# Preparing the first four delta rule heads in the front stage of a hybrid encoder layer, with keys projected later and wider steps

## Chip, cores and metric

The kernel runs on one core of one Trainium2 chip. The metric is device time in microseconds (us), the median of several runs. Engines are named as in the profile: PE is TensorE, PEld its weight load, DVE is VectorE, ACT is ScalarE, POOL is GpSimd, and SP issues most DMAs.

## What is computed

One bidirectional encoder layer over two sequences of 256 tokens, 512 rows in all, at width 1024. Three branches work side by side on the normalized input: a gated delta rule with 8 heads, latent attention (MLA) with 8 heads, and cross-attention with 4 heads into 256 memory tokens. Each is gated, projected to width 1024 and weighted by a sigmoid; the sum goes through `w_out`, and a final RMSNorm follows. Cut to what matters:

```python
h = rmsnorm(x, attn_norm_gain)
qkv, ab, z_gdn, cq, ckv, z_mla, q_mem, z_mem, gate_logits = split(h @ w_in)
q, k, v = split(silu(centred_conv(qkv, conv_w)))           # 5 taps
q, k = l2norm(q), l2norm(k)                                # per head
g, beta = -exp(a_log) * softplus(ab[0:2] + dt_bias), sigmoid(ab[2:4])
# delta rule, forward and backward, in chunks of 64 tokens:
lmat = (k*beta) @ k.T * decay, below the diagonal
t_inv = inverse(lmat + eye)
u, w = t_inv @ (v*beta), t_inv @ (k*beta*exp(gc))
for each chunk:
    v_new = u - w @ state
    o = (q*exp(g)) @ state + ((q @ k.T) * decay) @ v_new
    state = state*exp(g_last) + (k*exp(g_last - g)).T @ v_new
o_gdn = rmsnorm(o_fwd + o_bwd) * silu(z_gdn)
o_mla = mla(cq, ckv) * silu(z_mla)
o_mem = softmax(q_mem @ k_mem.T) @ v_mem * silu(z_mem)
merged = sum(sigmoid(gate_i) * (o_i @ w_branch_i))
y = rmsnorm(x + merged @ w_out, final_norm_gain)
```

## The kernel before, in words

Features lie on the 128 partitions and the 512 tokens along the free dimension. Each f32 operand of a large product is split into a rounded high part and a low rest, and the product is three passes on PE: high by high, high by low, low by high. `weight` (L190) loads a weight tile of 512 KB over SP, rounds it on ACT (`wh`, L200) and subtracts on DVE, or on POOL for the q, k and v tiles (`wl`, L204). `gemm` (L231) then runs 24 matmuls of 128x128 by 512 columns. `split` (L210, L212) does the same to activations.

There are three stages. The front stage (`front`, L1286) projects the memory keys and values, normalizes x, and runs the attention of the memory heads and of the eight MLA heads. In the attention of one head, s is a matmul (L281); DVE takes the maximum (L284, L290), ACT the exponential p (L295), DVE the reciprocal and the division of p (L298, L300); PE transposes p (pt, L304) and multiplies by v. Between these steps `fills(n)` takes whole tiles of other work from a list that `plan` (L1255) writes: projections of the delta rule's q, k and v with the convolution behind them (`qkv_tile`: five taps on DVE, L685 and L687, the last with SiLU), tokens of v transposed (`v_tokens`, with the copy vt on ACT, L710), merge gates g, output gates z.

The middle stage (`middle`, L1326) runs the delta rule. Its PE order is set by the program itself: `weave` drives several generators, which yield the PE time of a step and the time until the next is ready, and fills the gaps with tiles from what is left of the list. The generators are `preps`, `heads_load`, `heads_in`, two lanes of solves and `heads_out`. All other engines get an order from a scheduler that goes by priorities and its own clock.

`gdn_prep` (L714) prepares four heads at once: exponents of the decay (dr, ed, L735 to L742), products of keys in blocks of 32 (kd, 256 small matmuls, L753), norms, and the inverse of 32x32 blocks by a recurrence on DVE. That has 31 steps, each a product and a sum over the result of all steps before:

```python
nc.vector.tensor_tensor(t3, xx[:, i:i+1, 0:i].to_broadcast([P, i, i]), tt[:, 0:i, 0:i], op=ALU.mult)   # L800
nc.vector.tensor_reduce(tt[:, 0:i, i], t3, axis=AX.X, op=ALU.add)                                      # L802
```

Transposes (L810, L812) and copies on ACT to t32 (L823) and y32 (L826, L830) follow. In the middle stage of before, both groups of four heads are prepared there. For each head, `decay_in` and the exponentials of the decay e are made and multiplied with k by k (kk, L901; e, L912). `gdn_solve` then goes through a chain of small matmuls with copies between: p (L952) from t32, yp (L964), y (L977, L981), x (L995), u (L1005), xs (L1015), w (L1019), us (L1024), and the copies ub (L1010, L1027). `gdn_out` makes the output o (L1048) and its norm (so, L1064).

The back stage projects the delta rule's branch and multiplies by `w_out` (L1172); the last half row ends in a chain over DVE, ACT and POOL (L1178 to L1222).

At the very start, `mem_v` loads memT and the parameters prm. `add_square` (L241, L244) squares memT on ACT, and `split` multiplies it by a gain out of prm (mh, L210) for the first matmul vm (L358).

Of the kernel before, what the change touches and what calls it, by code (L numbers as in the profile page):

```python
# [7 lines left out]
F32 = mybir.dt.float32  # L8
F32R = mybir.dt.float32r
# [4 lines left out]
P = 128  # L14
# [140 lines left out]
class Layer:  # L155
# [16 lines left out]

    def ta(self, name):
        return self.pk.tile([P, 512], F32, tag="ta", bufs=2, name=name)
# [15 lines left out]
    def weight(self, src, n, name, pool=None):  # L190
# [9 lines left out]
        nc.scalar.activation(hi[:, :n], raw[:, :n], AF.Copy)  # L200
# [6 lines left out]
    def split(self, src, hi, lo, scale=1.0):  # L207

        nc = self.nc
        nc.scalar.activation(hi, src, AF.Copy, scale=scale)  # L210
        if isinstance(scale, float) and scale == 1.0:
            nc.vector.tensor_tensor(lo, src, hi.bitcast(F32), op=ALU.subtract)  # L212
        else:
            nc.vector.scalar_tensor_tensor(lo, src, scale, hi.bitcast(F32), ALU.mult, ALU.subtract)

# [110 lines left out]
    def mem_v(self):  # L326
# [6 lines left out]
        with self.tc.high_priority(offset=1000):  # L333
            for k in range(8):
                raw = self.pa.tile([P, 512], F32, tag="K", bufs=8, name=f"memT{k}")
# [8 lines left out]
        for k, (raw, wr) in enumerate(raws):  # L344
# [7 lines left out]
            self.split(raw, hl[:, 0], hl[:, 1], self.mg[:, k:k + 1])  # L352
# [7 lines left out]
            self.add_square(acc, raw, k, 1)  # L360
# [21 lines left out]
    def mem_kt(self, h):  # L382
# [5 lines left out]
            hi = self.pa.tile([P, 512], F32R, tag="K", bufs=8, name=f"kmh{h}")  # L388
            lo = self.pa.tile([P, 512], F32R, tag="K", bufs=8, name=f"kml{h}")
# [251 lines left out]
    def mla_qk(self, hh, between):  # L641
        A = self.A
        r = []
        for w, nk, xs, n, tag, bufs in ((A["w2"], 2, self.kl, "kn", "K", 8), (A["w3"], 3, self.ql, "qn", "Qn", 4)):
# [3 lines left out]
            hi = self.pa.tile([P, 512], F32R, tag=tag, bufs=bufs, name=f"{n}h{hh}")  # L648
            lo = self.pa.tile([P, 512], F32R, tag=tag, bufs=bufs, name=f"{n}l{hh}")
# [39 lines left out]
    def qkv_tile(self, h, part):  # L689
# [4 lines left out]
        if part < 2:  # L694
            if part == 0:
                self.kq[h] = self.pk.tile([P, 2, 2, 256], F32, tag="kq", bufs=8, name=f"kq{h}")
            self.conv(ps, f, self.kq[h][:, :, part], f"{f}")
            return
# [4 lines left out]
    def v_tokens(self, h):  # L703
# [6 lines left out]
        nc.scalar.activation(vt, vp, AF.Copy)  # L710
# [3 lines left out]
    def gdn_prep(self, g, kqs):  # L714
# [4 lines left out]
        nc = self.nc  # L719
        pg, c = self.pg, self.c  # L720
        h0 = 4 * g

# [23 lines left out]
        kp = self.ps_ms(0, f"kd{g}")  # L746
        for h in range(4):
            for s in range(2):
                for cc in range(2):
                    w = h * 4 + s * 2 + cc  # L750
                    for a in range(4):
                        t = slice(cc * P + 32 * a, cc * P + 32 * a + 32)
                        nc.tensor.matmul(kp[32 * a:32 * a + 32, 32 * w:32 * w + 32],  # L753
                                         kqs[h][:, s, 0, t], kqs[h][:, s, 0, t], start=True, stop=True)
# [37 lines left out]
        yield 1.8, 0.0  # L792
# [4 lines left out]
        for i in range(1, 32):  # L797
# [9 lines left out]
        if g:  # L807
            yield 0.0, 4.0
# [4 lines left out]
        if g:  # L813
            yield 0.0, 4.0


        t32 = pg.tile([P, 16, 32], F32, tag="t32", bufs=2, name=f"t32{g}")

        y32 = pg.tile([P, 32, 32], F32, tag="y32", bufs=2, name=f"y32{g}")
        for a in range(4):  # L820
# [3 lines left out]
            if g:  # L824
                yield 0.0, 1.5
        nc.scalar.activation(y32[:, 0:16], o2[:, :, 0:16].rearrange("p i u -> p u i"), AF.Copy)  # L826
        if g:
            yield 0.0, 2.5
        for q in range(2):
            nc.scalar.activation(y32[:, 16 + q:32:2], o1[:, :, 17 - q:32:2].rearrange("p i u -> p u i"), AF.Copy)  # L830
            if g:
                yield 0.0, 1.5
        self.ready[g] = self.now + (10 if g else 80)
# [37 lines left out]
    def gdn_in(self, hh):  # L871
# [8 lines left out]
        self.decay_exp(hh, 0, es[0])  # L880
        yield 0.0, 2.0
        self.decay_exp(hh, 1, es[1])
# [10 lines left out]
        yield 0.0, 6.0  # L893
# [24 lines left out]
    def gdn_solve(self, hh):  # L918
# [37 lines left out]
        nc.scalar.activation(p1s, p1[:, 0:128], AF.Copy, scale=-1.0)  # L956
        yield 0.32, 5.0
# [11 lines left out]
        def blk(i, f, g):  # L969
            return y[32 * f:32 * f + 32, i, :, 32 * g:32 * g + 32]  # L970


        for i in range(2):
            for q in range(2):
                d = q ^ i
                for f in (2 * q, 2 * q + 1):
# [515 lines left out]
```

## Time and profile before

| | us |
|---|---|
| median of 3 runs | 892.63 (892.06 to 894.81) |
| the profiled execution | 892.01 |
| its span | 890.2 |
| PE busy | 864.7 (97%) |
| PE weight load busy | 708.5 (80%) |
| DVE busy | 588.5 (66%) |
| ACT busy | 456.9 (51%) |
| POOL busy | 205.1 (23%) |

The profile is one execution; an engine is busy while it has an instruction in work. A row of the waits gives the waiting engine and line, then the engine and line it waited for, the sum in us, how often, and the longest. A row of a group gives line, engine, operation, output and inputs, shape and count, then busy us and the mean in ns, then the idle time just before and what ended it. A row of the timeline gives start, duration, engine and operation.

### The profile page before, as it was taken

Reading aid. Unit: us, or ns where it says so; the run is one execution under the profiler, and the core shown is the slowest. Engines: PE = TensorE matmul, PEld = TensorE weight load, DVE = VectorE, ACT = ScalarE, POOL = GpSimd, SP = SyncE. Lnnn points to the kernel's source line nnn. Section 1 sums busy time; section 2 is a strip of 40 time slices with the busy share of each in tenths; the row PEclk is TensorE's granted clock in tenths of the full one; section 3 lists DMA queues with packets and bytes.
Section 4 is the critical chain, followed back from the end, with each engine's and each line's share of the span. In section 5 each row is a group of like instructions: output and inputs, shape, how many; then the busy total and the mean of one; then the engine's idle time right before and its main releaser. Section 6 shows DMA issues by size and latency. Waiting matters only on the chain. (4 is left out here: it accounts for less than half of the span.)

```text
span 890.2 us, 13288 instructions
## 1 busy us (share of the span) xinstructions
PE 864.7 (97%) x4908; PEld 708.5 (80%) x4908; DVE 588.5 (66%) x992; ACT 456.9 (51%) x879; POOL 205.1 (23%) x150
## 2 busy tenths in 40 slices
PE   7999999999999999999998999999999999999996
PEld 5878886878888878887777877778888888888885
DVE  6775437876678775589996998775665544435642
ACT  6655455545554454456359557686665442213332
POOL 0230340121221310063330214422220001432121
PEclk9999999999999999999999999999999999999999
DMA  9322221542225423465341346434343337365332
GB/s 329 125 77 94 74 76 48 151 119 86 94 89 163 142 76 104 130 183 164 104 129 62 131 130 179 145 115 140 92 138 119 103 124 255 123 217 185 118 95 95
DMA packets 49313, 114.03 MB, mean 128 GB/s; under 512 B 6752, under 2 KB 12000, under 8 KB 49248
## 3 DMA queue, kind: packets, MB, share of 16 engines
q1 hardware_dynamic: 44496, 104.52, 37.5%
q10 hardware_dynamic: 4752, 8.65, 2.6%
q8 instruction: 39, 0.64, 0.3%
q14 instruction: 26, 0.21, 0.1%
HBM read 93.03 MB, written 16.97 MB: 124 GB/s over the span
## 5 line engine op out<-in xcount | busy, mean ns | idle before, releaser
L204 POOL TENSOR_TENSOR wl_qkv<-wr_qkv,wh_qkv 128x1024 fp32r<-128x1024 f32 x24 | 59.0, 2457 | 155.4 <-ACT wh_qkv L200 55.6
L685 DVE SCALAR_TENSOR_TENSOR kq<-cz,prm,kq 128x510 f32<-128x510 f32 (+1 forms) x64 | 54.2, 847 | 10.7 <-ACT kq L678 9.9
L231 PE MATMUL gm_qkv<-hh,wh_qkv 128*128 128x512 f32 x192 | 52.2, 407 | 3.2 <-DVE zt_z L1081 2.5
L231 PE MATMUL gm_g<-hh,wl_g 128*128 128x512 f32 x192 | 52.0, 400 | 0.0
L231 PE MATMUL gm_g<-hh,wh_g 128*128 128x512 f32 x192 | 51.9, 404 | 0.0
L231 PE MATMUL gm_qkv<-hh,wl_qkv 128*128 128x512 f32 x192 | 51.6, 405 | 0.0
L231 PE MATMUL gm_g<-hl,wh_g 128*128 128x512 f32 x192 | 51.3, 400 | 0.0
L231 PE MATMUL gm_qkv<-hl,wh_qkv 128*128 128x512 f32 x192 | 50.7, 399 | 0.0
L1142 POOL TENSOR_TENSOR mg<-mg,lg 128x512 f32<-128x512 f32 x16 | 29.0, 1814 | 79.4 <-DVE lg L1141 79.4
L231 PEld LDWEIGHTS gm_qkv<-hh,wh_qkv 128*128 128x128 f32 x192 | 35.3, 191 | 12.4 <-DVE zt_z L1081 3.2
L231 PEld LDWEIGHTS gm_qkv<-hl,wh_qkv 128*128 128x128 f32 x192 | 35.8, 188 | 8.6 <-issue 0.4
L231 PEld LDWEIGHTS gm_qkv<-hh,wl_qkv 128*128 128x128 f32 x192 | 35.8, 192 | 7.9
L231 PEld LDWEIGHTS gm_g<-hh,wh_g 128*128 128x128 f32 x192 | 35.3, 189 | 8.4 <-issue 0.5
L231 PEld LDWEIGHTS gm_g<-hh,wl_g 128*128 128x128 f32 x192 | 35.5, 189 | 7.7
L231 PEld LDWEIGHTS gm_g<-hl,wh_g 128*128 128x128 f32 x192 | 35.4, 189 | 7.8
L1172 PE MATMUL y<-wh_wo,mh 128*128 128x512 f32 (+1 forms) x144 | 40.0, 370 | 0.0
L200 ACT ACTIVATE wh_qkv<-wr_qkv 128x1024 fp32r<-128x1024 f32 x24 | 25.4, 1058 | 26.2 <-PE gm_qkv L231 6.5
L800 DVE TENSOR_TENSOR tm<-xx,tt 128x1 f32<-128x1 f32 (+30 forms) x62 | 37.0, 597 | 1.2
L204 DVE TENSOR_TENSOR wl_g<-wr_g,wh_g 128x1024 fp32r<-128x1024 f32 x24 | 31.3, 1306 | 9.4 <-PE gm_za L231 4.1
L200 ACT ACTIVATE wh_g<-wr_g 128x1024 fp32r<-128x1024 f32 x24 | 25.3, 1056 | 21.6 <-PE gm_g L231 12.7
L891 POOL TENSOR_TENSOR kl<-kq,kh 128x512 fp32r<-128x512 f32 x16 | 23.7, 1484 | 53.0 <-ACT kh L889 53.0
L685 DVE SCALAR_TENSOR_TENSOR vf<-cz,prm,vf 128x510 f32<-128x510 f32 (+1 forms) x32 | 29.6, 925 | 7.4 <-ACT vf L678 7.1
(403 smaller groups left out, 2263.2 us busy)
## 6 DMA issues: line engine op xcount, KB each, us to landing
wr_qkv<-in_w_dram SPq DMA_DIRECT2D x24, 512.0 KB, 3.5
wr_g<-in_w_dram SPq DMA_DIRECT2D x24, 512.0 KB, 3.6
e<-d_r SPq DMA_DIRECT2D x64, 96.0 KB, 3.5
wr_z<-in_w_dram SPq DMA_DIRECT2D x12, 512.0 KB, 3.6
wr_za<-in_w_dram SPq DMA_DIRECT2D x8, 512.0 KB, 3.4
d_g<-gt_g ACTq DMA_DIRECT2D x16, 256.0 KB, 2.0
wr_bm<-in_w_dram SPq DMA_DIRECT2D x8, 512.0 KB, 3.5
lg<-d_g SPq DMA_DIRECT2D x16, 256.0 KB, 3.4
```

What stands on the lines that cost most here:

```text
L200: nc.scalar.activation(hi[:, :n], raw[:, :n], AF.Copy)
L204: eng.tensor_tensor(lo[:, :n], raw[:, :n], hi[:, :n].bitcast(F32), op=ALU.subtract)
L231: nc.tensor.matmul(ps[:m], a[:, k * m:(k + 1) * m], xs[k][j], start=n == 0, stop=n == 3 * nk - 1)
L685: nc.vector.scalar_tensor_tensor(ys, zs, self.cw[:, f, m:m + 1], ys, ALU.mult, ALU.add)
L800: nc.vector.tensor_tensor(t3, xx[:, i:i + 1, 0:i].to_broadcast([P, i, i]), tt[:, 0:i, 0:i], op=ALU.mult)
L891: nc.gpsimd.tensor_tensor(lo, src, hi.bitcast(F32), op=ALU.subtract)
L1142: nc.gpsimd.tensor_tensor(self.merged[d], self.merged[d], gt, op=ALU.add)
L1172: nc.tensor.matmul(ps, xs[2 * j + q][a][:, t], b[:, q * 512 + c0:q * 512 + c1], start=j == 0 and n == 0, stop=j == 3 and n == 5)
```

## The change

Four things change.

The preparation of the first four heads now runs in the front stage. `front` makes the generator `prep0` ahead of the MLA heads and takes some steps of it behind each head from the second on, at lowered priority; the middle stage finishes it with the copies to t32 and y32. For this its pool pb is opened ahead of the front stage's pool, and some tiles of the front stage share tags in pb.

The list of fills has another order: k of heads 0 to 3 first, then q and v of these heads between gates; k of heads 4 to 7 is projected later, in the middle stage, and the second preparation waits for it.

The steps in the middle stage are spaced wider in the planner: 6.5 instead of 4.5 or 5.0 in the solve, 8 for 6 in `gdn_in`, 11 for 9 for the load of e; in the recurrence the spacing is narrower. Copies of y into blocks that need only y32 go ahead of yp; the copy vt gets a high priority; the exponentials come behind the last rounding of a weight.

At the two ends, the first square on ACT comes behind the rounding of mh, and in the last half row the product with the final gain moves from POOL to DVE, behind the row's factor r.

```diff
 def mem_v(self):
-            self.split(raw, hl[:, 0], hl[:, 1], self.mg[:, k:k + 1])
+            rnd = self.split(raw, hl[:, 0], hl[:, 1], self.mg[:, k:k + 1])
...
-            self.add_square(acc, raw, k, 1)
+            with self.tc.issue_after(rnd.ins) if k == 0 else nullcontext():
+                self.add_square(acc, raw, k, 1)
 def v_tokens(self, h):
-        nc.scalar.activation(vt, vp, AF.Copy)
+        with self.tc.high_priority(offset=2000):
+            nc.scalar.activation(vt, vp, AF.Copy)
 def gdn_prep(self, g):
+        with self.tc.high_priority(offset=0 if g else 900):
             for h in range(4):
...
+        yield 1.2, 0.0
...
         for i in range(1, 32):
...
-            if g:
-                yield 0.0, 2.0 + 0.005 * i * i
+            yield 0.0, 1.0 + 0.004 * i * i
...
+        if g == 0:
+            yield None
...
-        self.ready[g] = self.now + (10 if g else 80)
+        self.ready[g] = self.now + 10
 def gdn_in(self, hh):
-        self.decay_exp(hh, 0, es[0])
+        with self.tc.issue_after(self.wround):
+            self.decay_exp(hh, 0, es[0])
...
-        yield 0.0, 6.0
+        yield 0.0, 8.0
 def gdn_solve(...):
-        yield 0.32, 5.0
+        with self.tc.issue_after(first):
+            (copies of y32 into the blocks of y)
+            between(0)
+        yield 0.32, 7.0
...
-                yield 0.9, 4.5 if hh > 2 else 5.0
+                yield 0.9, 6.5
...
-            yield 0.45, 4.5 if hh > 2 else 5.0
+            yield 0.45, 6.5
 def output(self):
-            nc.gpsimd.tensor_tensor(y, y, fg[:, 512 + 256 * q:768 + 256 * q], op=ALU.mult)
+            if q == 0:
+                nc.gpsimd.tensor_tensor(y, y, fg[:, 512:768], op=ALU.mult)
...
-        nc.vector.tensor_scalar(ys[3][:, 512:1024], ys[3][:, 512:1024], r, None, ALU.mult)
+        nc.vector.tensor_scalar(ys[3][:, 512:768], ys[3][:, 512:768], r, None, ALU.mult)
+        nc.vector.scalar_tensor_tensor(y, y, r, fg[:, 768:1024], ALU.mult, ALU.mult)
 def plan(self):
-        self.fill += k[0:1] + qv(0) + k[1:2] + vt[0:1] + qv(1) + k[2:3] + vt[1:2] + k[3:4] + qv(2) + k[4:5] + vt[2:3]
-        self.fill += qv(3) + k[5:6] + vt[3:4] + k[6:]
+        self.fill += k[0:4] + qv(0) + vt[0:1] + g[0:1] + qv(1) + vt[1:2] + g[1:3] + qv(2) + vt[2:3] + g[3:4] + qv(3) + vt[3:4] + g[4:6]
+        self.fill += k[4:5] + g[6:7] + k[5:6] + g[7:8] + k[6:7] + g[8:9] + k[7:8] + z[0:1] + g[9:10] + z[1:2]
...
+    def prepare(self, n):
+        with self.tc.high_priority(offset=-300):
+            while n and next(self.prep0):
+                n -= 1
 def front(self):
+        self.prep0 = self.gdn_prep(0)
+        n = iter((5, 14, 6, 4, 4, 3, 99))
...
+                if g or h:
+                    self.prepare(next(n))
 def preps(self):
-        for g in range(2):
-            yield 0.0, 30.0 * g
-            self.pr[g] = yield from self.gdn_prep(g, [self.kq[4 * g + h] for h in range(4)])
+        self.pr[0] = yield from self.prep0
+        while any(h not in self.k_done for h in range(4, 8)):
+            yield 0.0, 1.0
+        self.pr[1] = yield from self.gdn_prep(1)
 def heads_load(self):
-            self.loaded[h] = self.now + 9.0
+            self.loaded[h] = self.now + 11.0
```

The lines of after are numbered 6 to 23 higher. Three places show what moved. The first is the start of ACT, with the semaphores that each instruction waits for (DMAHW2 is the landing of prm, DMAHW1 that of memT0); before:

```order
L338 DMA wr_vm0_87<-in_wvm_dram 128x512
L241 ACT_TABLE_LOAD
L241 ACTIVATE mem2_85<-memT0_86 128x512 [waits DMAHW1_49]
L210 ACTIVATE mh0_119<-memT0_86,prm_74 128x512 [waits DMAHW2_49]
L502 ACTIVATE expa_1213<-prm_74 128x16
L210 ACTIVATE mh1_139<-memT1_91,prm_74 128x512 [waits DMAHW3_49]
```

and after:

```order
L346 DMA wr_vm0_90<-in_wvm_dram 128x512
L215 ACT_TABLE_LOAD [waits DMAHW2_49]
L215 ACTIVATE mh0_118<-memT0_89,prm_74 128x512 [waits DMAHW1_49]
L247 ACTIVATE mem2_88<-memT0_89 128x512
L511 ACTIVATE expa_1208<-prm_74 128x16
L215 ACTIVATE mh1_138<-memT0_89,prm_74 128x512 [waits DMAHW3_49]
```

The rounding mh0 stands ahead of the square mem2, and the load of the function tables, which waited for nothing, now stands behind the wait for prm.

The second is DVE in the front stage at the sixth MLA head (a50 and a51 are its two halves); before:

```order
L284 TENSOR_REDUCE mx_a51_3184<-s_a51_3173 128x2
L1081 SCALAR_TENSOR_TENSOR za5_3080<-za5_3080,gm_za5_3087 128x512
L290 SCALAR_TENSOR_TENSOR nb_a51_3186<-mx_a51_3184,rq_896 128x2
L204 TENSOR_TENSOR wl_kn7_3251<-wr_kn7_3247,wh_kn7_3249 128x256
L212 TENSOR_TENSOR qnl6_3131<-gm_qn6_3120,qnh6_3130 128x512
L298 RECIPROCAL rs_a51_3192<-sm_a51_3189 128x2
L300 TENSOR_SCALAR p_a51_3188<-p_a51_3188,rs_a51_3192 128x256 x2
```

and after:

```order
L290 TENSOR_REDUCE mx_a51_3317<-s_a51_3306 128x2
L1103 SCALAR_TENSOR_TENSOR za5_3213<-za5_3213,gm_za5_3220 128x512
L821 TENSOR_TENSOR tm0_3555<-xx0_2422,tt_2122 128x900
L306 TENSOR_SCALAR p_a50_3283<-p_a50_3283,rs_a50_3287 128x256 x2
L209 TENSOR_TENSOR wl_kn7_3404<-wr_kn7_3400,wh_kn7_3402 128x256
L217 TENSOR_TENSOR qnl6_3264<-gm_qn6_3253,qnh6_3263 128x512
L296 SCALAR_TENSOR_TENSOR nb_a51_3319<-mx_a51_3317,rq_891 128x2
L823 TENSOR_REDUCE tt_2122<-tm0_3555 128x30
L821 TENSOR_TENSOR tm0_3705<-xx0_2422,tt_2122 128x961
L304 RECIPROCAL rs_a51_3325<-sm_a51_3322 128x2
L823 TENSOR_REDUCE tt_2122<-tm0_3705 128x31
L306 TENSOR_SCALAR p_a51_3321<-p_a51_3321,rs_a51_3325 128x256 x2
```

The last steps of the recurrence (tm0 and tt) now stand between the maximum, the scaled maximum nb and the division of p.

The third is PE at the end of the last head's solve (us71) and the start of its output (o7); before, with the twelve matmuls of be7 cut to those at the ends:

```order
L1024 MATMUL us71_7311<-w271_7284,y1_3558 128x128 x2
L231 MATMUL gm_g27_7274<-hh6_361,wl_g27_7272 128x512
L231 MATMUL gm_g27_7274<-hh7_368,wl_g27_7272 128x512
L231 MATMUL gm_be7_7326<-xe0_6001,wh_be7_7322 128x512
...
L231 MATMUL gm_be7_7326<-xe3_6007,wl_be7_7324 128x512
L1048 MATMUL o7_7345<-e70_6547,ub7_7069 128x256
```

and after:

```order
L1037 MATMUL xs71_7288<-u271_7243,m1_3723 128x128 x2
L237 MATMUL gm_be7_7285<-xe2_6279,wh_be7_7281 128x512
...
L237 MATMUL gm_be7_7285<-xe3_6281,wl_be7_7283 128x512
L273 MATMUL rob6_7311<-cst_292,ro6_7261 128x128 x4
L1046 MATMUL us71_7320<-w271_7291,y1_3722 128x128 x2
L1070 MATMUL o7_7329<-e70_6449,ub7_7024 128x256
```

Fourteen large matmuls stood between us71 and o7; now none does.

More of the change, by code (lines that the diff above doesn't have):

```diff
@@ L1 @@
-from contextlib import ExitStack
+from contextlib import ExitStack, nullcontext
 import numpy as np
@@ L171, in ps_ms, with big @@
         return self.ps.tile([P, 512], F32, tag=f"ms{par}", bufs=2, name=name)
+    def big(self, i, name, dt=F32R):
+        t, n = ("blk", 3) if i < 3 else ("tt", 1)
+        return self.pb.tile([P, 2, 512], dt, tag=t, bufs=n, name=name)
     def ta(self, name):
@@ L967, in gdn_solve @@
                                      start=True, stop=True)
[L969 to L976, printed above, removed]
-                    nc.scalar.activation(blk(i, f, f), y32[32 * f:32 * f + 32, 16 * d + 4 * h:16 * d + 4 * h + 4], AF.Copy)
         for i in range(2):
```

114 lines of the change are left out of this document (64 added, 50 removed).

## The prediction

> **What bounds the kernel now.** I read the profile's page first: the busy shares, and TensorE's busy tenths in 40 slices.
>
> ```profile
> span 890.2 us, 13288 instructions
> PE 864.7 (97%) x4908; PEld 708.5 (80%) x4908; DVE 588.5 (66%) x992; ACT 456.9 (51%) x879; POOL 205.1 (23%) x150
> ...
> PE   7999999999999999999998999999999999999996
> ```
>
> TensorE is busy for 864.7 of 890.2 us, so 25.5 us is all that better order can win as long as the matmuls stay the same, and the change leaves them the same. Its weak slices are the first, the last and the 22nd. Then the waits of TensorE (waiting line, line waited for: us in total, times, longest), and busy time by stretches (start:end, length, then busy time and instructions of TensorE, its weight load, VectorE, ScalarE and GpSimd, granted clock, DMA share, GB/s):
>
> ```profile
> PE vm L358 <- ACT mh L210: 5.8, 1, 5.8
> PE p L952 <- ACT t L823: 2.7, 2, 1.8
> PE gm_qkv L231 <- DVE zt_z L1081: 2.5, 2, 1.6
> PE us L1024 <- ACT vt L710: 1.6, 1, 1.6
> PE pt_a L304 <- DVE p_a L300: 1.5, 2, 1.3
> PE kk L901 <- DVE e L912: 1.4, 1, 1.4
> ```
>
> ```profile
> 250.00:350.00 100.00, 98.63 (x493) 81.97 (x492) 74.12 (x116) 50.30 (x95) 19.86 (x10) 1.00 0.40 120
> 400.00:500.00 100.00, 97.29 (x662) 77.49 (x661) 88.92 (x188) 60.35 (x113) 24.80 (x20) 0.98 0.38 122
> 500.00:600.00 100.00, 93.58 (x594) 76.75 (x593) 85.14 (x134) 69.46 (x148) 33.71 (x29) 1.00 0.45 138
> 600.00:875.00 275.00, 275.00 (x1567) 226.95 (x1566) 139.26 (x213) 115.64 (x229) 57.40 (x44) 1.00 0.44 140
> ```
>
> So there is nothing to win after 600 us. Of the 25.5 us, 5.8 lie at the start, 1.4 between 250 and 350, 2.7 between 400 and 500, 6.4 between 500 and 600, and about 7 behind the last matmul. The change touches all five places.
>
> **The wait of the first solves (gain).** Matmul p of heads 0 and 1 (L952) waits for t32, the last product of the first preparation. Finer windows around it:
>
> ```profile
> 466.00:468.00 2.00, 1.08 (x6) 0.51 (x5) 2.00 (x5) 1.97 (x4) 0.11 (x1) 1.00 0.63 225
> 468.00:470.00 2.00, 0.25 (x4) 0.14 (x4) 1.92 (x6) 1.95 (x3) 1.16 (x1) 1.00 0.37 103
> 470.00:472.00 2.00, 1.98 (x61) 1.73 (x62) 0.00 (x0) 1.97 (x8) 0.00 (x0) 0.64 0.07 28
> 472.00:474.00 2.00, 2.00 (x6) 1.52 (x6) 0.00 (x0) 1.99 (x3) 0.00 (x0) 0.51 0.03 8
> ```
>
> The idle time is 0.92 + 1.75 + 0.02 = 2.69 us, and right behind it the granted clock falls to 0.64 and 0.51, which costs 0.36 x 2 + 0.49 x 2 = 1.70 us more. The Trainium skill (TensorE: Matmul & The Clock Gate, "What's actually happening") has the clock halve after an idle window of about 3.4 us, by which a pause below that length would cost only itself, and this term would be −2.7. The trace differs: 2.69 us of idle in two pauses were enough. With the first preparation done in the front stage, only its copies to t32 and y32 stand in the middle stage, on ScalarE well ahead of the solves, and the wait goes with its clock: −4.4 us. What is late next there would be kk and na of head 0, which do not wait in before; bounds −2.7 (the clock dips elsewhere) to −4.4.
>
> **The waits of the middle (gain).** The 6.4 us idle between 500 and 600 us are the waits on zt_z (2.5), vt (1.6), e (1.4) and some of 0.5 and less. All are work of VectorE or ScalarE that stands behind other work while the second preparation runs its 31-step recurrence. The costs of this, for both preparations together (line, engine, operation, count | busy, mean ns):
>
> ```profile
> L800 DVE TENSOR_TENSOR tm<-xx,tt 128x1 f32<-128x1 f32 (+30 forms) x62 | 37.0, 597 | 1.2
> L802 DVE TENSOR_REDUCE tt<-tm 128x1 f32<-128x1 f32 (+30 forms) x62 | 31.0, 501 | 1.3
> L810 DVE STREAM_TRANSPOSE o<-tt 128x1024 f32<-128x1024 f32 x2 | 2.5, 1240 | 0.0
> ```
>
> One recurrence is (37.0 + 31.0)/2 = 34.0 us, dependent step on dependent step. Taking one out of the middle stage lets the second start earlier; each solve step gets 1.5 to 2 us more distance in the planner (4.5 or 5 to 6.5), the exponentials of e are asked for 2 us earlier (9 to 11), and the copy of vt moves to the head of ScalarE's queue. The big waits are so addressed one by one. I keep 1.4 of 6.4: four keys' convolutions now come into this stage, at 4 x 4.2 us of VectorE, worked out as five steps of 0.847 for a tile, of which this row has four (the second row is used below):
>
> ```profile
> L685 DVE SCALAR_TENSOR_TENSOR kq<-cz,prm,kq 128x510 f32<-128x510 f32 (+1 forms) x64 | 54.2, 847 | 10.7 <-ACT kq L678 9.9
> L204 DVE TENSOR_TENSOR wl_g<-wr_g,wh_g 128x1024 fp32r<-128x1024 f32 x24 | 31.3, 1306 | 9.4 <-PE gm_za L231 4.1 <-PE gm_g L231 3.5 <-issue 1.0
> ```
>
> So −5.0 us; bounds 0 (the same waits under other names) and −6.4.
>
> **The front stage (loss).** There the attention of a head runs s, softmax on VectorE and ScalarE, transposes on TensorE; the wait of pt_a on p_a (L300) is the sign that VectorE came late. VectorE was busy 74.1 of the 100 us from 250 to 350. Now the recurrence (34.0), two transposes like L810 (2.5) and, as I estimate, some 4.5 us of smaller steps come in: 41. Two tiles of convolution leave it (8.4) and two gate tiles' subtractions come (2 x 1.3): 74.1 + 41 − 8.4 + 2.6 = 109 us of work in 100. But a step may start under the end of a neighbour that it does not depend on:
>
> ```profile
> 300.71 0.68 DVE L737 TENSOR_TENSOR ed<-ngcl,cst 128x512 f32<-128x512 f32 x1
> 301.31 0.68 DVE L212 TENSOR_TENSOR qnl<-gm_qn,qnh 128x512 fp32r<-128x512 f32 x1
> ```
>
> The second begins 0.08 us before the first ends. The 62 steps of the recurrence depend on each other, but now stand between others; at 0.08 for each that is 5 us, so 104 us. Low priority only decides the order in which the instructions are queued; in the queue a step of 0.5 to 1.4 us stands in front of p_a and nb_a, and TensorE waits behind those. I take +3.5 us of these 4, mostly at heads 4 to 6, where the steps are longest. Bounds: −1.4 (nothing lost, and the pt_a wait goes too) to +9 (all of the excess).
>
> **The start (loss).** ScalarE's first operations, and the parameters prm (issue row: KB, us to landing):
>
> ```profile
> 1.18 0.42 SPq L341 DMA_DIRECT2D prm<-in_prm_dram  x1
> ...
> 1.18 1.28 ACT L241 ACT_TABLE_LOAD   x1 [1.18 <-PEq L1481]
> ...
> 4.50 0.63 ACT L241 ACTIVATE mem<-memT 128x512 f32<-128x512 f32 x1 [2.04 <-DMA memT<-in_memT_dram]
> 5.04 0.70 ACT L210 ACTIVATE mh<-memT,prm 128x512 fp32r<-128x512 f32 x1
> ```
>
> ```profile
> prm<-in_prm_dram SPq DMA_DIRECT2D x1, 87.0 KB, 3.7
> ```
>
> In before the table load (1.28 us) runs at 1.18, under the loads, and mh ends at 5.74, when the first matmul starts (5.80). The change puts mh ahead of the square, and the first instruction on ScalarE is now the one that needs prm: in the new order the table load itself carries that wait. prm lands at 1.18 + 3.7 = 4.9. Then load to 6.2, mh to 6.9, first matmul at 6.9: +1.1. If the load were not held, mh could start at 4.9 without the square before it: −0.1, the other bound. The Trainium skill (ScalarE: Activation LUTs, "What ACT_TABLE_LOAD costs") adds a drain of about 1.38 us to each switch; by it this term would be about +2.5 and the forecast 889.4. The trace speaks against it, since after a later load the next operation starts 0.01 us behind:
>
> ```profile
> 110.44 1.28 ACT L507 ACT_TABLE_LOAD   x1
> 111.73 0.26 ACT L507 ACTIVATE dec<-dec 128x64 f32<-128x64 f32 x1
> ```
>
> **The last head's output (loss).** In before 14 big matmuls stand between us of head 7 and its output o; now o stands directly behind us, and needs the copies ub of ScalarE:
>
> ```profile
> L1027 ACT ACTIVATE ub<-us 64x256 f32<-64x256 f32 x32 | 12.1, 378 | 8.9 <-PE us L1024 8.3
> ```
>
> Two of 0.378 in a row: +0.7 us (bounds 0.4 to 1.0).
>
> **The tail (gain).** Behind the last matmul a chain of small steps runs:
>
> ```profile
> 884.28 0.21 DVE L1215 TENSOR_SCALAR yss<-yss 128x1 f32<-128x1 f32 x1 [0.58 <-ACT jk L1180]
> 884.33 0.72 POOL L1216 TENSOR_TENSOR y<-y,fg 128x256 f32<-128x256 f32 x1 [1.90 <-ACT jk L1180]
> 885.01 0.55 POOL L1218 TENSOR_TENSOR fr<-yss,cst 128x1 f32<-128x1 f32 x1
> 885.59 0.72 ACT L1219 ACTIVATE y<-y,fr 128x512 f32<-128x512 f32 x1 [1.34 <-POOL fr L1218]
> 885.59 0.49 DVE L1221 TENSOR_SCALAR y<-y,fr 128x512 f32<-128x512 f32 x1 [1.09 <-POOL fr L1218]
> ```
>
> GpSimd's product y x fg stands ahead of fr and goes to VectorE behind it. Then fr can start at about 884.5 instead of 885.01: −0.5 us. VectorE's last part grows by a second operation of some 0.3, but ScalarE's operation of 0.72 is the longer of the two in before and covers it; bounds −0.5 to −0.2.
>
> **At nothing.** The pool pb opened earlier and the tiles shared by tags cost no instruction; the preparation issues no DMA, so SP's queue is moved past nothing; four keys' weight subtractions move along GpSimd's queue, which was busy 19.9 of 100 us in the front and 33.7 in the stretch that takes them.
>
> **The sum.** −4.4 − 5.0 + 3.5 + 1.1 + 0.7 − 0.5 = −4.6 us. The profiled execution took 892.01 us (span 890.2 and 1.8 around it), so 887.4; the median of the three timed runs is 892.63, 0.6 above it. The forecast is 888.0 us. Over the bounds of the two large unknowns, its own range is 884.5 to 891.
>
> **The rivals.** First, VectorE takes over the front stage (slower). The mechanism: in the fixed queue the recurrence's steps delay p_a of heads 4 to 6, TensorE waits at each pt_a and s_m, and pauses of 2 us and more close together halve the clock, as they did at 466 us. For it: the 109 of 100 above. Against it: in the stretch from 400 to 500 VectorE was busy for 88.9 with the same recurrence inside, and TensorE lost only p's 2.7. Price: all of the 9 us excess, and three closings of the clock at 1.7: +14.1 in place of +3.5 us, so 888.0 + 10.6 = 898.6. It makes the kernel slower from a front loss of 3.5 + (895.3 − 888.0) = 10.8 us on. Without the clock it is 888.0 + 5.5 = 893.5, no change. Chance 0.16.
>
> Second, the waits of the middle only change their names (no change): VectorE stays near full from 400 to 600, since the keys' convolutions replace the recurrence that left, and the waits return at other matmuls. Then the 5.0 is not had: 888.0 + 5.0 = 893.0. For it: busy time is moved, not removed. Against it: 34 us leave this stage and 4 x 4.2 = 17 come. Chance 0.20.
>
> Third, the front hides all of it: −1.4 in place of +3.5 and all of the middle's waits but 0.4 gone: 888.0 − 4.9 + 1.0 = 884. For it: the softmax work has slack at heads 0 to 3. Against it: the sum above 100. Chance 0.10.
>
> **How the numbers follow.** The forecast has 0.54, the rivals 0.16, 0.20 and 0.10. What a measurement can tell from no change is 0.3% or 2.7 us: faster is below 889.95, slower above 895.3. Of the forecast's 0.54, 0.04 lie above 889.95. Faster is 0.50 + 0.10 = 0.60; the same is 0.04 + 0.20 = 0.24; slower is 0.16. The range from 882.5 to 895.5 takes in forecast, second and third rival with their spread of some 2 us, and leaves out the first.
>
> **What would show it.** In the new profile the wait of p on t and the clock below 1.00 near 470 us are gone; the waits of zt_z, vt and e between 500 and 600 sum to under 2 us; between 250 and 350 VectorE is busy for 95 or more and TensorE idles 3 to 6 us, mostly at pt_a or s_m behind p_a or nb_a; the first matmul starts at 6.9; a new wait of o on ub of about 0.7; GpSimd's fr starts directly behind yss. The prediction is wrong if TensorE's idle time between 250 and 350 passes 10 us or stays under 1, if granted clock falls below 1.00 in the front, or if the waits between 400 and 600 sum to more than 5.

## The result and the profile after

The changed kernel takes 897.74 us, median of 5 runs (896.66 to 899.75), beside 892.63 before: a ratio of 1.0056, 95% interval 1.0036 to 1.0075. It is slower by 5.1 us, where 888.0 was forecast. The profiled execution of it took 899.75 us, the slowest of the five and 2.0 above their median; its span is 7.8 us longer than that of before.

The page, and the waits of TensorE, after:

```profile
span 898.0 us, 13279 instructions
PE 868.4 (97%) x4908; PEld 709.8 (79%) x4908; DVE 580.8 (65%) x993; ACT 458.0 (51%) x879; POOL 201.6 (22%) x149
```

```profile
PE vm L366 <- ACT mh L215: 7.1, 1, 7.1
PE kk L920 <- DVE e L931: 3.8, 4, 1.6
PE gm_g L237 <- ACT cz L689: 2.3, 2, 1.3
PE gm_g L237 <- ACT gt_g L1129: 2.0, 1, 2.0
PE pt_a L310 <- DVE p_a L306: 1.2, 1, 1.2
PE gm_qkv L237 <- ACT gt_g L1129: 1.2, 1, 1.2
```

The wait of p on t is gone, and so are those on zt_z and vt. In their place stand kk on e, gates on cz and on gt_g. The stretches say where the time lies:

```profile
250.00:350.00 100.00, 95.59 (x458) 77.91 (x457) 86.90 (x165) 43.05 (x79) 17.92 (x8) 0.98 0.34 106
295.00:350.00 55.00, 50.59 (x238) 40.72 (x237) 50.77 (x83) 21.97 (x43) 10.20 (x5) 0.97 0.26 88
400.00:410.00 10.00, 8.03 (x28) 6.10 (x27) 1.11 (x2) 9.70 (x21) 7.08 (x8) 0.83 0.71 196
400.00:500.00 100.00, 98.03 (x713) 78.42 (x712) 76.83 (x156) 66.55 (x142) 36.18 (x27) 0.98 0.38 126
430.00:620.00 190.00, 183.47 (x1318) 149.47 (x1317) 150.12 (x275) 127.57 (x273) 57.27 (x41) 1.00 0.37 121
500.00:600.00 100.00, 95.11 (x629) 78.12 (x629) 73.00 (x119) 68.99 (x143) 31.76 (x27) 1.00 0.43 135
600.00:700.00 100.00, 98.36 (x649) 81.82 (x648) 56.24 (x106) 56.89 (x132) 16.51 (x18) 1.00 0.37 122
700.00:880.00 180.00, 179.97 (x856) 146.49 (x855) 84.34 (x102) 57.33 (x88) 36.22 (x23) 1.00 0.46 151
```

From 250 to 350 us TensorE idles 4.41 us, 1.37 in before, all of it from 295 on. All 1.97 us of idle time from 400 to 500 lie in its first ten, with the clock at 0.83. From 500 to 700 it idles 4.89 + 1.64 = 6.53 us; in before it was 6.42, all ahead of 600. Two places need more detail, first the front stage at its worst, with the operations of POOL, DVE and PE there:

```profile
320.57 2.38 POOL L209 TENSOR_TENSOR wl_qkv<-wr_qkv,wh_qkv 128x1024 fp32r<-128x1024 f32 x1 [6.03 <-ACT wh_qkv L205]
320.88 2.49 DVE L306 TENSOR_SCALAR p_a<-p_a,rs_a 128x256 f32<-128x256 f32 x2
...
323.16 0.81 PE L310 MATMUL pt_a<-cst,p_a 128*128 128x128 f32 x4 [1.22 <-DVE p_a L306]
```

```profile
320.00:324.00 4.00, 2.78 (x15) 1.95 (x13) 4.00 (x7) 2.40 (x5) 2.38 (x1) 1.00 0.02 5
324.00:328.00 4.00, 2.66 (x9) 1.88 (x9) 4.00 (x8) 1.80 (x5) 0.00 (x0) 0.81 0.53 169
328.00:332.00 4.00, 4.00 (x14) 3.16 (x14) 3.25 (x7) 0.42 (x1) 0.00 (x0) 0.76 0.02 8
```

Two divisions of p_a take 2.49 us together, beside a subtraction of GpSimd; TensorE waits 1.22 for them and idles 1.34 in the next stretch of 4, and the clock closes, that is, the granted clock falls, to 0.81 and 0.76: 4 x 0.19 + 4 x 0.24 = 1.7 us more. Then ScalarE ahead of the wait at 404 us:

```profile
394.79 2.03 PE L237 MATMUL gm_g<-hh,wl_g 128*128 128x512 f32 x8
...
395.36 4.65 ACT L843 ACTIVATE t<-o 32x512 f32<-32x512 f32 x4
...
400.02 1.16 ACT L845 ACTIVATE y<-o 128x512 f32<-128x512 f32 x1
401.07 1.24 ACT L848 ACTIVATE y<-o 128x256 f32<-128x256 f32 x2
402.20 1.15 ACT L908 ACTIVATE kh<-kq 128x512 fp32r<-128x512 f32 x2
403.24 0.63 ACT L699 ACTIVATE cz<-kq 128x512 f32<-128x512 f32 x1
403.76 0.59 ACT L1129 ACTIVATE gt_g<-gm_g 128x512 f32<-128x512 f32 x1
...
404.40 3.28 PE L237 MATMUL gm_g<-hh,wh_g 128*128 128x512 f32 x8 [1.97 <-ACT gt_g L1129]
```

The copies to t32 and y32 run as one block of 7 us, with kh and cz behind it. The gate's activation, which frees the PSUM tile of the next projection, comes last, at 403.76; the last matmuls of that gate had ended at 396.8.

### The profile page after: what moved, and what is told of

It reads as the page before. It is cut to its first block, busy times and chain, and to the rows that moved or that the text cites. A ratio compares the mean times of both kernels' runs of the same rounds, so it can differ in the third digit from the quotient of the medians.

```text
span 898.0 us, 13279 instructions
## 1 busy us (share of the span) xinstructions
PE 868.4 (97%) x4908; PEld 709.8 (79%) x4908; DVE 580.8 (65%) x993; ACT 458.0 (51%) x879; POOL 201.6 (22%) x149
## 4 chain that ended last, share of the span: by engine, by line
PE 79%; DVE 10%; ACT 4%; DMA 3%; issue 2%; POOL 1%; SPq 0%; ACTq 0%; POOLq 0%; DVEq 0%
PE gm_g L237 13%; PE gm_qkv L237 10%; PE gm_bm L237 5%; PE gm_z L237 5%; PE gm_bg L237 5%; PE y L1195 4%; PE gm_za L237 4%; PE vm L366 3%; PE gm_be L237 3%; PE gm_qm L237 3%; PE gm_km L237 3%; PE gm_cq L237 2%; PE s_a L287 2%; PE o L1070 2%; PE kk L920 2%
## 5 line engine op out<-in xcount | busy, mean ns | idle before, releaser
L237 PE MATMUL gm_g<-hh,wh_g 128*128 128x512 f32 x192 | 53.7, 411 | 4.2 <-ACT cz L689 2.3
L910 POOL TENSOR_TENSOR kl<-kq,kh 128x512 fp32r<-128x512 f32 x16 | 21.7, 1361 | 67.1 <-ACT kh L908 46.4
L237 PE MATMUL gm_bm<-xa,wh_bm 128*128 128x512 f32 x128 | 33.2, 399 | 0.0
```

The lines of the kernel that those rows point to most:

```text
L237: nc.tensor.matmul(ps[:m], a[:, k * m:(k + 1) * m], xs[k][j], start=n == 0, stop=n == 3 * nk - 1)
L910: nc.gpsimd.tensor_tensor(lo, src, hi.bitcast(F32), op=ALU.subtract)
```

## The experiments

Ratios are to the kernel before, run beside it, with 95% intervals; the changed kernel as it was made has 1.0056. Times and idle times of a trace are those of one execution, the profiled one. My theory from the profile: the loss has several separate parts (the start, VectorE in the front stage, the copies on ScalarE), and the middle stage's waits were never about the work that was moved. The rivals stand with each run.

### The start

```diff
-            with self.tc.issue_after(rnd.ins) if k == 0 else nullcontext():
-                self.add_square(acc, raw, k, 1)
+            self.add_square(acc, raw, k, 1)
```

> The changed kernel, with the first square on ScalarE ahead of the rounding of mh again, as before the change; nothing else. Theory (the start costs on its own: the table load waits for prm, and the later first matmul also meets a colder clock): first matmul at 5.8 us instead of 7.1, TensorE's lag at 25 us 1.9 us smaller, median 897.7 - 1.9 = 895.8. Rival (the first matmul waits for memT and prm anyway, so the order on ScalarE is worth at most the square): first matmul 0.2 us earlier or less, median 897.7.

Measured: 1.0028 (1.0017 to 1.0038), 2.5 us less than the changed kernel; the wait of the first matmul is 5.8 us again. By the ratios the edit at the start costs 2.5 us, by my estimate from the two intervals some 2 us either way; 1.3 us of it are the wait itself. The row of the table load in the changed kernel says how:

```profile
4.99 1.28 ACT L215 ACT_TABLE_LOAD   x1 [4.99 <-DMA prm<-in_prm_dram]
6.28 0.72 ACT L215 ACTIVATE mh<-memT,prm 128x512 fp32r<-128x512 f32 x1
```

### The copies on ScalarE

The copies of the first group are ordered behind the gate tile g06:

```diff
+            with nullcontext() if g else self.tc.issue_after(self.gts[0, 6]):
                 nc.scalar.activation(t32[r], ...
```

> The changed kernel, with the copies to t32 and y32 of the first four heads ordered on ScalarE behind the activation of the gate tile g06. Theory (the wait of gm_g on gt_g at 404 us and the half clock behind it come from gt_g standing behind these 7 us of copies): the wait of 2.0 us and the clock of 0.83 between 400 and 410 us go, TensorE's lag does not rise by 3.7 us there, median 897.7 - 3.7 = 894.0. Rival (ScalarE is full at that place whatever the order): another wait of about 2 us within 20 us, p on t or kk on kh, and the median stays at 897.7.

Measured: 1.0018 (1.0007 to 1.0028), 3.4 us less. The stretch in which TensorE idled:

```profile
400.00:410.00 10.00, 10.00 (x44) 8.04 (x43) 1.10 (x2) 9.98 (x19) 6.52 (x12) 1.00 0.65 195
```

ScalarE is as full as in the changed kernel (9.98 of 10 us, 9.70 there) and TensorE loses nothing: it was the order alone.

### Both mendings

> The changed kernel with both mendings, the square on ScalarE as before the change and the copies to t32 and y32 behind the gate tile g06. Theory (the two losses are independent and add): ratio to before 1.0056 - 0.0028 - 0.0038 = 0.999, about 892. Rival (the two were measured against a noise of that size and one of them does not add): ratio 1.002 or more.

Measured: 1.0007 (0.9997 to 1.0017). The sum of the two would be 0.999; within the intervals they add. With two orders on ScalarE mended, the change is worth nothing against before, some 5 us short of the forecast.

### The front stage without the recurrence

```diff
         for i in range(1, 32):
-            tm = ...
+            if g:
+                tm = ...
```

> The changed kernel without the 31 steps of the first recurrence: part of the computation (the inverse of the 32x32 blocks of heads 0 to 3) is left out. It prices the 34 us of VectorE in the front stage. Theory (VectorE full in the front stage is what makes TensorE lose there): TensorE's idle time between 250 and 350 us falls from 4.4 us to under 1.5, the clock there is 1.00, median 897.7 - 5.5 = 892.2. Rival (the new order of the projections in the front stage costs it): idle time stays over 3 us, median 896 to 898.

Measured: 0.9943 (0.9927 to 0.9959), 10.1 us less than the changed kernel; 5.5 were expected. The front stage:

```profile
250.00:350.00 100.00, 100.00 (x509) 83.64 (x508) 67.78 (x110) 50.64 (x90) 17.13 (x10) 1.00 0.39 118
```

No idle time and no closed clock, so the loss there is the recurrence's and not the new order of the projections. The wait at 404 us went as well, since the copies came earlier (at 388.9 us in place of 395.4). And from 430 to 620 us TensorE idles 3.21 us in place of 6.53, so not all of the 10 us is the front stage's.

### Later, and earlier

Of the steps of the first recurrence 23 now stand ahead of the fifth head, and 8 behind the last (with both mendings; `mark` is the last head's division of p):

```diff
-        n = iter((5, 14, 6, 4, 4, 3, 99))
+        n = iter((5, 14, 10, 0, 0, 0, 99))
...
+            with self.tc.issue_after(self.mark) if i > 23 and not g else nullcontext():
```

> As the kernel with both mendings, and of the 31 steps of the first recurrence 23 stand ahead of the fifth MLA head and 8 behind the last one; none between heads 4 and 7. Theory (the front stage loses time where steps of the recurrence stand between the work of heads 4 to 6 on VectorE; from 350 to 425 us VectorE has room): TensorE's idle time between 295 and 350 us falls from 4.4 us to 1.5 or less with the clock at 1.00, ratio 0.999 - 0.005 = 0.994, about 887. Rival (it only moves the loss: p of head 0 then waits for t32, or heads 0 to 3 lose what heads 4 to 6 gain): ratio 0.998 to 1.002, with a wait of p on t of 2 us or more, or one before 295 us.

Measured: 0.9997 (0.9983 to 1.0011), so mostly the rival: from 295 to 350 us 3.05 us of idle time are left though no step stands between the heads, and two new waits of kk on e appear behind the place where the last steps now stand, about 414 us. Then all steps ahead of the fifth head, begun one head earlier:

```diff
-        n = iter((5, 14, 6, 4, 4, 3, 99))
+        n = iter((5, 9, 9, 9, 1, 1, 1, 99))
...
-                if g or h:
-                    self.prepare(next(n))
+                self.prepare(next(n))
```

> The kernel with both mendings, and the first preparation begun one MLA head earlier, with all 31 steps of its recurrence ahead of the fifth MLA head: nothing of it stands between the work of heads 4 to 7 and nothing late in front of the solves. Theory (the loss lies where steps of the recurrence compete with the attention heads 4 to 6; from 190 to 295 us VectorE has room): TensorE's idle time from 295 to 350 us falls from 4.4 us to 1, no wait over 1 us from 380 to 420, ratio 1.0007 - 0.009 = 0.992, about 885.5. Rival (34 us of VectorE cost TensorE the same wherever they stand in the front stage): the loss moves to 230 to 300 us, ratio 0.998 to 1.002.

Measured: 0.9952 (0.9938 to 0.9966), 4.9 us better than both mendings alone, where 8 were hoped for. The place matters, but by less than the time says. Both mendings alone, then the earlier preparation:

```profile
295.00:350.00 55.00, 50.61 (x233) 40.69 (x232) 49.60 (x81) 22.11 (x44) 9.15 (x5) 0.94 0.27 90
295.00:350.00 55.00, 52.44 (x265) 43.19 (x264) 43.82 (x66) 28.10 (x52) 8.90 (x5) 1.00 0.28 93
```

Idle time is 2.56 us in place of 4.39, but 0.44 us is new ahead of 295. The clock of 1.00 in place of 0.94 is worth 0.06 x 55 = 3.3 us in these two executions, and from 400 to 500 us the 1.16 us of idle time are gone too. What is left in the front is mostly one wait of pt_a on p_a, 2.2 us, though the recurrence's last step has ended by 313.9 us. Ahead of that division a step of the convolution took 2.36 us beside a subtraction on GpSimd:

```profile
317.39 2.41 POOL L209 TENSOR_TENSOR wl_qkv<-wr_qkv,wh_qkv 128x1024 fp32r<-128x1024 f32 x1 [5.15 <-PE gm_za L237]
317.98 2.36 DVE L697 SCALAR_TENSOR_TENSOR kq<-cz,prm,kq 128x508 f32<-128x508 f32 x1
...
321.98 0.81 PE L310 MATMUL pt_a<-cst,p_a 128*128 128x128 f32 x4 [2.15 <-DVE p_a L306]
```

### The middle stage

The second recurrence left out, as a price of its 34 us on VectorE:

> The changed kernel without the 31 steps of the second recurrence: part of the computation (the inverse of the 32x32 blocks of heads 4 to 7) is left out. It prices the 34 us of VectorE in the middle stage. Theory (the waits between 500 and 610 us come from the order of the solve's steps and from two PSUM tiles for kk, not from a full VectorE): the waits of kk on e, 3.8 us in 4, stay at 2.5 or more, ratio to before 1.0056 - 0.003 = 1.003. Rival (VectorE is full there, as the prediction had it): the waits of kk go to under 1 us, ratio 0.998 or less.

Measured: 1.0057 (1.0039 to 1.0075), no gain, which fits my theory by the time. But the waits went the other way: kk on e went from 3.8 to 1.4 us, and one wait of a gate on cz grew to 4.7, at 471 us, behind the second group's copies, which again ran in one block on ScalarE. From 500 to 600 us TensorE idled nothing, 4.89 us in the changed kernel. So the time alone is inconclusive, and the next run adds the two mendings and holds these copies back:

```diff
-            with nullcontext() if g else self.tc.issue_after(self.gts[0, 6]):
+            with self.tc.issue_after(self.wround if g else self.gts[0, 6]):
```

> The kernel with both mendings, without the 31 steps of the second recurrence (part of the computation is left out: the inverse of the blocks of heads 4 to 7), and with the copies of the second preparation ordered on ScalarE behind the weight rounding issued last, so that they can't pile up early as they did at 466 us in the run before. Theory (the second recurrence on VectorE sets the waits between 480 and 620 us, and that run only gave the gain back to the pile of copies on ScalarE): TensorE's idle time from 430 to 620 us falls from 6.5 us in the changed kernel to 2 or less, ratio 1.0007 - 0.006 = 0.995. Rival (these waits come from the spacing and the two PSUM tiles for kk whatever VectorE does): idle time over 5 us, ratio 1.000.

Measured: 0.9959 (0.9944 to 0.9974), 0.0048 or 4.3 us below the kernel with both mendings:

```profile
430.00:620.00 190.00, 189.04 (x1391) 155.93 (x1391) 121.00 (x219) 131.33 (x280) 55.56 (x45) 1.00 0.41 128
```

Idle time is 0.96 us, 6.04 with both mendings and 6.53 in the changed kernel. The waits between 500 and 610 us come from the second recurrence, the one that the change leaves where it was; my theory on kk's two PSUM tiles falls. How they come is not shown: in the changed kernel the last step of that recurrence starts at 531.2 us and all 6.53 us of idle time lie behind it, so it seems to cost by the work that it has put off.

### The spacing

The old spacing in the changed kernel (4.5 for 6.5 in the solve and so on):

> The changed kernel with the old spacing of the solve's steps, of the load of e and of kk (4.5 or 5, 9 and 6). Theory (the wider spacing does gain, and the waits between 500 and 600 us are what is left): the waits there rise from 5.9 to 8 us or more, median 900. Rival (spacing is worth nothing; the waits there come from VectorE being full): the same sum of waits within 1.5 us, median 897.7. A second rival (wider spacing itself delays the chain of heads): fewer waits, median 895.

Measured: 1.0188 (1.0164 to 1.0212), 11.8 us worse than the change as made; 2 were expected. And the new spacing in the kernel before:

> The kernel before, with the wider spacing of the change alone (6.5 for 4.5 or 5, 7 and 7.5 for 5 and 5.5, 8 for 6, 11 for 9). Theory (the wider spacing by itself takes away waits of the solves, 12 us in the changed kernel): the waits between 500 and 600 us fall from 6.4 to 3 or less, ratio 0.995, about 888. Rival (in the order of before the spacing is not what sets these waits, and a longer chain of heads ends later): ratio 1.000 or above.

Measured: 1.0143 (1.0123 to 1.0163), 12.8 us worse than before; a gain was expected. In the first case TensorE idles 11.34 us from 500 to 700 us, at a clock of 0.97 there. Neither spacing serves the other order. The stretch that loses most in the second case is the end of the last solves, which lost nothing in before:

```profile
700.00:880.00 180.00, 174.67 (x927) 143.56 (x926) 87.77 (x121) 65.39 (x120) 39.52 (x28) 0.97 0.43 142
```

```profile
PE so L1064 <- DVE sq L1060: 2.5, 1, 2.5
```

Its 5.33 us of idle time and 0.03 x 180 = 5.4 us of clock make up most of the 12.8. The first us of the solves starts at 501.8 us (494.6 in before), the last at 756.4 (740.5), so the wider chain ends late; as I read it, too few other matmuls are left there to fill its gaps. The same came of 9 in place of 6 between the halves of kk, on top of the earlier preparation:

> As the run before, with 9 instead of 6 in the planner between the two halves of kk of a head. Theory (kk waits on e since its two PSUM tiles are read by eight operations of VectorE in between, and the planner allows too little): the waits of kk on e fall from 4 to 5 us to under 1.5, ratio 0.004 below the run before. Rival (the longer chain of heads costs as much, as the wider spacing did in the kernel before): ratio the same or higher, with a wait at the end of the middle stage.

Measured: 1.0112 (1.0093 to 1.0130). The waits of kk on e are gone, as the theory had it, but a wait of so on sq of 4.4 us appears near 747 us and one of xs on ub of 4.2. In the narrow case kk on e grew from 3.8 to 6.7 us; what makes these waits longer was not followed further.

### GpSimd beside VectorE

The subtraction on GpSimd beside the slow p_a asked for a run of its own. All low parts of weights on VectorE, on top of the earlier preparation:

```diff
-        eng = nc.gpsimd if name[0] == "q" or name == "km3" else nc.vector
+        eng = nc.vector
```

> As the kernel with the earlier preparation, with the subtractions of the weights' low parts all on VectorE, none on GpSimd (the 24 tiles of q, k and v and a few more). It asks why single operations of VectorE take 1.2 to 2.5 us instead of 0.35 to 0.75. Theory (VectorE stands still while GpSimd runs an operation with two inputs from the same memory): the mean of the convolution's step kq falls from about 0.88 us to under 0.79, and that of tm from 0.65 or so to under 0.6, though VectorE gets some 30 us more work. Rival (it is transfers into the memory that slow VectorE): the means stay. For the time no strong expectation: 30 us more on VectorE against 25 us of standing still, ratio 0.99 to 1.01.

Measured: 0.9869 (0.9848 to 0.9890), 881.52 us: better than both kernels, and by 0.0083, or 7.4 us, better than the run with the earlier preparation. VectorE's groups:

```profile
L697 DVE SCALAR_TENSOR_TENSOR kq<-cz,prm,kq 128x510 f32<-128x510 f32 (+1 forms) x64 | 48.4, 756 | 8.1 <-ACT kq L690 7.5
L821 DVE TENSOR_TENSOR tm<-xx,tt 128x1 f32<-128x1 f32 (+30 forms) x62 | 31.6, 510 | 0.7
L209 DVE TENSOR_TENSOR wl_qkv<-wr_qkv,wh_qkv 128x1024 fp32r<-128x1024 f32 x24 | 29.3, 1222 | 28.7 <-ACT wh_qkv L205 19.1 <-PE gm_qkv L237 5.6 <-ACT p1s L978 2.3
```

The convolution's step takes 756 ns on the mean (928 in the run with the earlier preparation, 847 in before), tm 510 (590 and 597), and a subtraction 1222 here against 2457 on GpSimd in before. The same edit alone in the changed kernel and in the kernel before, side by side:

> The changed kernel as it is, with only the subtractions of the weights' low parts moved from GpSimd to VectorE. If the front stage loses because VectorE stands still beside GpSimd (theory): TensorE's idle time from 295 to 350 us falls from 4.4 us to 2 or less, though the recurrence stays where the change put it; what is left to the change is the start and the copies on ScalarE; ratio to before 1.0056 - 0.010 = 0.995. If it is the place of the recurrence alone (rival): idle time 4 us or more there, ratio 1.000 or above.

> The kernel before, with only the subtractions of the weights' low parts moved from GpSimd to VectorE. Theory (the collisions cost the kernel before as well, in the convolutions and the recurrences, 10 us in all): ratio 0.990, and the changed kernel beside it still slower by the start and the copies, about 5 us. Rival (only the changed kernel, with a full VectorE in the front, gains): ratio 0.998 to 1.003; then the change is worth a gain once GpSimd is out of the way.

Measured: 0.9945 (0.9928 to 0.9963) for the changed kernel and 0.9934 (0.9917 to 0.9951) for that of before. In the stretch that decides, the changed kernel and then that of before:

```profile
295.00:350.00 55.00, 53.37 (x270) 44.05 (x269) 51.16 (x94) 26.46 (x50) 0.00 (x0) 1.00 0.29 96
```

```profile
295.00:350.00 55.00, 55.00 (x292) 46.57 (x291) 36.86 (x69) 26.86 (x53) 0.00 (x0) 1.00 0.36 116
```

The idle time of the changed kernel there falls from 4.41 to 1.63 us and the clock stays open, with the recurrence in the same place and VectorE as busy (51.16 for 50.77). So a good part of the front's loss needs both, the recurrence there and GpSimd's subtractions; the rest is the recurrence alone. The edit takes away the collisions and halves a subtraction's time at once, and the runs don't separate these two. Without GpSimd's subtractions the change as made is worth nothing either way that these intervals can tell. With the two mendings and the earlier preparation it is worth something: 0.9869 beside the 0.9934 of before, both without GpSimd's subtractions, and 0.9952 with them.

## Why the prediction was wrong, point by point

**The wait of the first solves: right.** p no longer waits, and the clock near 470 us is open. The 4.4 us came.

**The waits of the middle: the step that failed.** "−5.0 us" for the 6.4 idle between 500 and 600 came out as no gain: 6.53 us from 500 to 700, 6.42 in before. I took 34 us of VectorE out of the stage as a whole and let that pay for waits at one place of it. VectorE did get freer, 73.0 of the 100 us from 500 to 600 for 85.1, and TensorE's waits stayed, under other names. In the changed kernel it is the second recurrence, which was not moved, that makes them; without it and with its copies held back, 0.96 us was left from 430 to 620. The second rival's result was right and its reason was not, since VectorE did not stay near full. Whether the keys' convolutions have a part in it, no run tells.

**The copies at the start of the middle stage: priced at nothing, cost 3.4 us.** The prediction said that they "stand in the middle stage, on ScalarE well ahead of the solves". I asked who needs the copies, not what is queued behind 7 us of them. The answer was the activation that frees a projection's PSUM tile; 1.97 us of idle time followed and, in the profiled execution, 10 x 0.17 = 1.7 us of half clock. The 3.4 us are what ordering the copies gave back.

**The front stage: right in kind, too small, and in part for another reason.** 3.5 us were forecast, 3.04 more idle time and 1.7 of clock came in the profiled execution, with bounds of −1.4 and 9. But VectorE was busy for 86.9 of 100 us and not 95: the account of 104 of 100 was too high, and the loss is no matter of a full engine. The recurrence has 30.9 us in that window, near the 34.0, but 15.0 us of convolution steps are gone from it (31.8 to 16.8), where 8.4 were reckoned. The loss sits in single places. Some 2.6 of the 4.41 us lie near 320 us, where a subtraction on GpSimd holds VectorE up for 2 us and p_a comes late, with two waits right behind it; in the run without the recurrence the same subtractions cost TensorE nothing there. Waits on gt_g (1.2 us, near 303) and on qnh (0.7, near 347) are most of the rest, which I have not followed. The first rival's mechanism, clock included, happened once and not three times. Its 898.6 is near the measured 897.7, but the rest of that is the copies and the start.

**The start: right, and a little small.** The first matmul waits 7.1 us; 6.9 was forecast. The matmuls behind it also run slowly for longer: the group vm<-wl_vm that starts at 23.91 us in before starts at 25.84, 1.93 us later, of which 1.26 are the wait. The time gained by undoing it was 2.5 us, with an interval that holds both. The drain that the Trainium skill (ScalarE: Activation LUTs, "What ACT_TABLE_LOAD costs") adds didn't show: mh starts 0.01 us behind the load.

**Output of the last head, and the tail: nothing.** From 700 to 880 us TensorE idles 0.03 us, so the 0.7 us for the copies ub did not come. In the tail GpSimd's fr starts sooner, as forecast:

```profile
891.15 0.42 DVE L1201 TENSOR_TENSOR y<-y,y 128x256 f32<-128x256 f32 x1 [1.42 <-PE y L1195]
...
892.44 0.55 POOL L1242 TENSOR_TENSOR fr<-yss,cst 128x1 f32<-128x1 f32 x1 [2.14 <-DVE yss L1238]
...
893.80 0.33 SPq L1247 DMA_DIRECT2D out_dram<-y  x1
```

fr comes 1.29 us behind the last addition of y, 1.72 in before. But the span ends 4.2 us behind the issue of the last transfer, at 898.0, and 6.85 us behind that addition; in before it is 6.91, so 0.06 us of the 0.5 came. Whether a shorter tail would show over several runs was not tried alone.

Against the sum, in the two profiled executions: −4.4 as forecast, +0.1 for −5.0, +4.7 for +3.5, +1.9 for +1.1, +3.7 for 0, and about 0 both for the +0.7 of the last output and for the −0.5 of the tail. That is +6.0 us. The spans differ by 7.8; the other 1.8 us I have not followed.

Of the prediction's own signs of being wrong, two came: the granted clock in the front fell below 1.00 (0.98 from 250 to 350 us), and TensorE idled 1.97 + 4.89 = 6.86 us between 400 and 600, more than 5. Two of its sums were wrong as well. Its bounds for the middle and the front taken together reach from 881.7 to 898.5, not from 884.5 to 891, so they hold the measured time. And the third rival, which takes away more of the middle's waits, should be 1.0 us lower for that and not higher: about 882.

## What to carry to other kernels

When work is moved out of a stage, first find which part of the stage's work makes each wait; a stage's busy share does not say it. Cost a moved block on the queue that it lands in by what stands behind it, above all by whatever frees a PSUM tile, and not by when its own result is needed. A planner's spacing belongs to one order of the work: after a move it has to be found again, and it can't be carried back.

## What the runs showed that I had not expected

Some of VectorE's operations all but stand still beside a subtraction on GpSimd. Here is a small step of the recurrence in the changed kernel, and the next, larger one, which runs alone:

```profile
283.14 2.41 POOL L209 TENSOR_TENSOR wl_qkv<-wr_qkv,wh_qkv 128x1024 fp32r<-128x1024 f32 x1 [10.64 <-PE gm_qkv L237]
283.25 2.37 DVE L821 TENSOR_TENSOR tm<-xx,tt 128x49 f32<-128x49 f32 x1
...
285.89 0.23 DVE L821 TENSOR_TENSOR tm<-xx,tt 128x64 f32<-128x64 f32 x1
```

Two operations of p_a took 2.49 us beside one of 2.38 us on GpSimd; over the trace their mean is 432 ns, this pair included:

```profile
L306 DVE TENSOR_SCALAR p_a<-p_a,rs_a 128x256 f32<-128x256 f32 x32 | 12.5, 432 | 0.4
```

Moving the subtractions onto VectorE, some 40 us of them (29.3 for q, k and v, the rest smaller groups), raised its busy time only from 582 to 587 us and made the kernel 7.4 us faster. The Trainium skill ("SBUF — State Buffer", section "SBUF: two separate sides") says that the two engines share a pair of ports: a GpSimd operation that reads SBUF and a VectorE operation with two inputs in SBUF, or in a mode that uses both ports, shut each other out for a whole instruction. The runs agree, and the prediction should have used it: it costed VectorE's work by mean durations that held these collisions already, and did not ask what GpSimd would be doing beside the new steps.

TensorE's clock closed after 1.22 + 1.34 us of idle time between 320 and 328, and again after a single wait of 1.97 us at 404; in before it closed after 2.69 us. Pauses of the same length did not always do it. In the run with the old spacing TensorE idles 1.25 + 1.34 us between 320 and 328, and the clock there is 1.00. It also stays at 1.00 behind a wait of 2.0 us near 400 with the square moved back, one of 2.0 with the old spacing and one of 1.9 without the second recurrence, and behind the 2.2 us near 322 with the earlier preparation. So a closing and its 1.7 us belong to one execution; the length of a pause does not settle it, and no run here shows what does.
